# Stick-breaking attention by pairs of query blocks, and a sigmoid without GpSimd and reciprocal

## Chip, cores and metric

One core of one Trainium2 chip runs the whole program. The metric is the device time of one execution in microseconds (us); a difference is judged on the median of several runs.

## What is computed

Two layers of a streaming encoder are run on 512 prompt rows and 32 later rows ("sample") together, so 544 columns in all, with a model width of 1024. Each layer projects the residual stream into four token mixers: stick-breaking attention, retention, forgetting attention ("fox") and an indexer-selected sparse attention ("dsa"). The four results are gated, summed and projected ("merge"), then normalised, and a feed-forward network of width 2816 follows. The change touches two mixers. Cut to what matters:

```python
# stick-breaking, 4 heads of 64; 'earlier' is key position < query position
z = q @ k.T / 8
log_1mb = where(earlier, log_sigmoid(-z), 0)
after   = cumsum over keys from the end (log_1mb) - log_1mb
w       = where(earlier, exp(log_sigmoid(z) + after), 0)
y       = w @ v
# retention: the result of each head, normalised, is multiplied by a gate
y_ret = head_norm(retention(q, k, v)) * silu(ret_g)      # silu(x) = x * sigmoid(x)
```

## The kernel before

The stream is held as 128 rows by 272 columns, two halves of them, each value split into a high and a low part in a shorter float format (`split`, L694), so that a product is three matmuls of 272 columns. Most large projections use a seven-product scheme on 2 by 2 blocks (`strassen`, L784); its weight blocks are split by ScalarE (high part) and by VectorE or GpSimd (low part). A string of seven letters says which of the two makes each low part: `v` VectorE, `g` GpSimd. `SPLITS[3]` (L101) is the string for `proj2` (L919), which makes the value projection of retention, one call a layer.

**Who sets the order.** Nothing is issued in the order of the code. Every call becomes an operation with a modelled duration and a priority (its place in the code, less an offset); a list scheduler (`Plan.schedule`, L553) plays the five engines and takes on each the ready operation of highest priority. The addresses of the tiles in the on-chip memory are fitted to the lifetimes that such a play gives (`Memory.places`, L202), for several settings, of which the best by the plan is taken; an operation whose tile lies on bytes of an older one waits for the older one's readers. Where the plan sees TensorE idle, dummy matmuls of a tile called `idle` are put in (L635). So any change of an operation gives a new order of everything behind it. In the profile all operations have the line of the loop that issues them (L659, L657 for the dummies), so the rows are read by tile names.

**Banks.** The eight PSUM banks have fixed users (L107): `z`, two banks, holds the scores of all mixers; `d`, four banks, the projections; `a` the weighted sums of values; `p` transposes.

**Stick-breaking** (`stick`, L1434). The loop at L1439 takes the four query blocks of 128 in turn, and for each the two head parities `s`. The key blocks up to the query's own are taken from the last to the first, in units of up to two. A unit fills one `z` bank: a mask matmul where it holds the diagonal block, then for each key block and each of two heads two matmuls of 128 columns (L1458, high and low part of the keys). `stick_unit` (L1421) makes the log terms: Abs, Exp and Ln on ScalarE, one operation on VectorE, then the split into `hl` by ScalarE and GpSimd. Cumulative sums are matmuls into the same bank (L1467): of a block with itself by a triangle (`trin`), with every later key block by minus ones (`onen`), two parts each, 256 columns. A last Exp on ScalarE makes the weights `sw`, and after both parities the products with the values go to bank `a` (L1480), j from 0 up, for each head in turn. A unit also places two steps of the top-k selection of the dsa mixer (L1462), VectorE work on the tile `score`. After the four blocks one more unit serves the sample rows.

**Retention's gate** (`silu`, L1553). For each of two row blocks and two column halves, a projection lies in a `d` bank; ScalarE makes exp(-x) into `se`, GpSimd adds 1, VectorE takes the reciprocal, and VectorE multiplies with the bank's x into `sg`, which frees the bank.

Of the kernel before, what the change touches and what calls it, by code (L numbers as in the profile page):

```python
# [14 lines left out]
AF = mybir.ActivationFunctionType  # L15
OP = mybir.AluOpType
# [81 lines left out]
GROUPS = ((0, 6), (6, 8), (14, 8))  # L98
CORNER = ("vv",) * 12
PIECES = ([(0, 512, "v"), (512, 1024, "v")], [(0, 512, "a"), (512, 768, "a"), (768, 1024, "g")], [(0, 1024, "v")])  # L100
SPLITS = ("vvvvvvv", "vvvvvvv", "vvvvvvv", "vgvgvgv")  # L101
RESIDUAL = 2
SLACKS = (400, 100, 0)
FITS = ((10.0, 5.0), (5.0, 5.0), (10.0, 2.0), (10.0, 10.0))
# [560 lines left out]
class Build:  # L665
# [253 lines left out]
    def proj2(self, col, names):  # L919
# [3 lines left out]
        at = lambda c, h: out[:, c, h * HB:(h + 1) * HB]  # L923
        ps = self.strassen(r, 4, self.xt, None, SPLITS[3], "d", (at(0, 1), at(1, 0), at(1, 1)))[0]
        self.ev(at(0, 0), ps, eng="s")
# [508 lines left out]
    def stick(self, q, qb, k, svt):  # L1434
        nc = self.nc
        ks = self.k_parts(k, "sk")
        v, vs = svt
        y = self.fm("y_sb")
        for i in range(4):  # L1439
            blocks = list(range(i, -1, -1))  # L1440
            units = [tuple(blocks[a:a + 2]) for a in range(0, len(blocks), 2)]
            W = {}
            for s in range(2):
                r = slice(s * 64, s * 64 + 64)
                later = []
                for un in units:
                    n = 256 * len(un)
                    z = self.tps("sz")
                    first = True
                    if i in un:  # L1450
                        nc.tensor.matmul(z[:, :256], self.B["ident"],
                                         self.B["sbmask"][:, None, :].to_broadcast([128, 2, 128]), start=True,
                                         stop=False, skip_group_check=True)
                        first = False
                    for x, j in enumerate(un):
                        for p in range(2):
                            c = (2 * x + p) * 128
                            self.z(z[:, c:c + 128], q, ks, 2 * p + s, slice(i * 128, (i + 1) * 128),  # L1458
                                   slice(j * 128, (j + 1) * 128), first, True)
                            first = False  # L1460
                    hl = self.stick_unit(z, n)
                    self.select(SELECT[1])  # L1462
                    own = [(hl, 256 * x) for x in range(len(un))]
                    for x, j in enumerate(un):
                        for src, a, lhs in [(*own[x], self.trin)] + [(*b, self.onen) for b in later + own[:x]]:
                            for part in range(2):
                                nc.tensor.matmul(z[:, 256 * x:256 * x + 256], lhs, src[:, part, a:a + 256], start=False,  # L1467
                                                 stop=True, skip_group_check=True)
                    later = later + own
                    w = self.w512("sw")  # L1470
                    nc.scalar.activation(w[:, :n], z[:, :n], AF.Exp)
                    for x, j in enumerate(un):
                        W[s, j] = (w, 256 * x)
            o = self.aps("so")
            for p in range(2):
                for s in range(2):
                    h = 2 * p + s
                    for j in range(i + 1):
                        w, a = W[s, j]
                        nc.tensor.matmul(o[:, h * 128:(h + 1) * 128], v[:, j, p * 128:(p + 1) * 128],  # L1480
                                         w[:, a + p * 128:a + (p + 1) * 128], start=j == 0, stop=j == i)
            self.ev_heads(y, o, i * 128, 128)

        kc = self.cache_k("cache_sb_k", 384, NKS)
        nc.vector.tensor_copy(kc[:, :, PAST:NKS], k[:, :, T:NT])
        vc = self.cache_v("cache_sb_v", 256)
        nc.vector.tensor_copy(vc[:32, 2, :], vs)
        z = self.tps("szs")
        nc.tensor.matmul(z[:, 256:384], self.B["ident"], self.B["sbmask_s"], start=True, stop=False,
                         skip_group_check=True)  # L1490
        for j in range(3):
            for p in range(2):
                c = j * 128 + p * 64
                nc.tensor.matmul(z[:, c:c + 64], kc[:, p, j * 128:(j + 1) * 128], qb[:, p].rearrange("r s q -> r (s q)"),
                                 start=False, stop=True, skip_group_check=True)
        hl = self.stick_unit(z, 384)
        for j in range(3):
            for b in range(j, 3):
                for part in range(2):
                    nc.tensor.matmul(z[:, j * 128:(j + 1) * 128], self.trin if b == j else self.onen,  # L1500
                                     hl[:, part, b * 128:(b + 1) * 128], start=False, stop=True, skip_group_check=True)
        w = self.w512("sws")
        nc.scalar.activation(w[:, :384], z[:, :384], AF.Exp)
        self.pv_sample(w.rearrange("p (b q) -> p b q", q=128), lambda kr, j, p: vc[:kr, j, p * 128:(p + 1) * 128], y, 128)
        return y
# [35 lines left out]
    def retention(self):  # L1541
        nc, l = self.nc, self.l
        cs = self.fm("cs")
        a, b = CONST_AT["cos"][0], CONST_AT["sin"][1]
        nc.sync.dma_start(cs.rearrange("p a b -> p (a b)"), self.consts_dram[:, a:b])
        q = self.rotary(self.proj(COL["ret_q"], "rq0"), cs)
        k = self.rotary(self.proj(COL["ret_k"], "rk0", 0.125), cs)
        vf = self.proj2(COL["ret_v"], "rv")
        v, vs = self.tm(vf, "rvt", True, None)
        sg = self.fm("sg")  # L1550
        se = self.fm("se")

        def silu(c, h, ps):  # L1553
            cs = slice(h * HB, (h + 1) * HB)
            nc.scalar.activation(se[:, c, cs], ps, AF.Exp, scale=-1.0)
            nc.gpsimd.tensor_scalar(se[:, c, cs], se[:, c, cs], 1.0, None, op0=OP.add)
            nc.vector.reciprocal(se[:, c, cs], se[:, c, cs])
            nc.vector.tensor_tensor(sg[:, c, cs], se[:, c, cs], ps, op=OP.mult)

        for c in range(2):  # L1560
            a = COL["ret_g"] + c * 128
# [3 lines left out]
        y = self.fm("y_ret")  # L1565
# [39 lines left out]
        for c in range(4):  # L1605
            cc = slice(c * 128, (c + 1) * 128)
            A = self.w512("A", (128, 2, 2, 128))
            for s in range(2):
                r = slice(s * 64, s * 64 + 64)
                z = self.tps("rz")  # L1610
# [9 lines left out]
            o = self.aps("ro")  # L1620
            for p in range(2):
                if c:
                    nc.tensor.matmul(o[:, p * 128:(p + 1) * 128], qd[:, p], S[:, p], start=True, stop=False)
                for s in range(2):
                    h = 2 * p + s
                    nc.tensor.matmul(o[:, h * 64:(h + 1) * 64], A[:, s, p], v[:, c, h * 64:(h + 1) * 64],
                                     start=not c, stop=not c or s == 1)
# [10 lines left out]
        z = self.tps("rzs")  # L1638
        for p in range(2):
            nc.tensor.matmul(z[:32, p * 64:(p + 1) * 64], k[:, p, T:NT], qb[:, p].rearrange("r s q -> r (s q)"),  # L1640
                             start=True, stop=True)
# [9 lines left out]
        o = self.aps("ros")  # L1651
        for p in range(2):
            nc.tensor.matmul(o[:32, p * 128:(p + 1) * 128], qd[:, p], S[:, p], start=True, stop=False)
            for s in range(2):
                h = 2 * p + s
                nc.tensor.matmul(o[:32, h * 64:(h + 1) * 64], A[:32, p, s], vs[:, h * 64:(h + 1) * 64], start=False,
                                 stop=s == 1)
# [430 lines left out]
```

## Time and profile before

| what | us |
|---|---|
| median of 3 runs (lowest to highest) | 1942.51 (1942.05 to 1944.62) |
| the profiled execution, its own time | 1938.36 |
| span of the profiled execution, first to last instruction | 1936.6 |
| TensorE busy | 1871.6 |
| VectorE busy | 1607.1 |
| ScalarE busy | 1053.3 |
| GpSimd busy | 498.8 |

The profile comes from one execution. PE is TensorE, DVE is VectorE, ACT is ScalarE, POOL is GpSimd. Matmuls are pipelined: a matmul's record lasts longer than the time until the next one starts, so the price of one in a row of many is taken here from start to start. The dummy matmuls count as busy.

### The profile page before, as it was taken

The numbers are of one execution on the slowest core, as the hardware profiler recorded it, in microseconds if no ns is written. First come the engines' busy times: TensorE is split into PE (matmuls) and PEld (weight loads), VectorE is DVE, ScalarE is ACT, GpSimd is POOL, SyncE is SP. The second block draws the span as 40 slices with busy tenths as digits, with TensorE's granted clock in tenths as the row PEclk, the third lists the DMA queues.
The fourth block names the chain that finished last, engine by engine and source line by source line (L and its number), as shares of the span: only waits on it lengthen the run. The fifth ranks groups of instructions, "written<-read, shape, count | busy, mean of one in ns | idle before, by whom it ended". The sixth has DMA issues, their size and how long they took to land.

```text
span 1936.6 us, 39257 instructions
## 1 busy us (share of the span) xinstructions
PE 1871.6 (97%) x14658; PEld 1815.8 (94%) x14658; DVE 1607.1 (83%) x3566; ACT 1053.3 (54%) x2183; POOL 498.8 (26%) x500
## 2 busy tenths in 40 slices
PE   9999999999999999999999999999999999999997
PEld 8998898999999999999989989999999999999996
DVE  5988768887879989988789796687788799899875
ACT  4465533555637656556465563365556475565552
POOL 0343031143441111321413421312434301114101
PEclk9999999999999999999999999999999999999999
DMA  8222243667542587776413222346665237777741
GB/s 229 79 64 81 55 101 75 153 142 163 145 124 77 135 195 174 170 180 169 130 23 95 60 84 68 78 107 159 151 154 155 86 86 169 188 174 175 171 114 47
DMA packets 387423, 241.38 MB, mean 125 GB/s; under 512 B 27272, under 2 KB 363576, under 8 KB 386976
## 3 DMA queue, kind: packets, MB, share of 16 engines
q1 hardware_dynamic: 361888, 193.78, 36.2%
q0 software_dynamic: 25344, 45.10, 13.8%
q8 instruction: 115, 1.88, 0.4%
q14 instruction: 76, 0.62, 0.1%
HBM read 183.69 MB, written 7.82 MB: 99 GB/s over the span
## 4 chain that ended last, share of the span: by engine, by line
PE 71%; DVE 17%; DMA 5%; ACT 4%; issue 3%; POOL 1%; SPq 1%; POOLq 0%; ACTq 0%; DVEq 0%
PE bank L659 70%; DVE wop L659 3%; DMA ws<-wa 3%; DVE lnw L659 2%; DVE y L659 2%; DVE wsum L659 1%; DVE wlo L659 1%; DVE st L659 1%; DVE q L659 1%; DVE score L659 1%; DVE fu L659 1%; SPq L659 1%; DVE su L659 0%; DVE sv L659 0%; ACT wop L659 0%
## 5 line engine op out<-in xcount | busy, mean ns | idle before, releaser
L659 PE MATMUL bank<-T,wop 128*128 128x272 f32 x3456 | 460.6, 289 | 4.6 <-DVE su L659 3.1
L659 PEld LDWEIGHTS bank<-T,wop 128*128 128x128 f32 x3456 | 443.3, 188 | 7.1 <-DVE su L659 4.3
L659 PE MATMUL bank<-h0hi,wop 128*128 128x272 f32 x1152 | 244.9, 291 | 0.3 <-DVE acc L659 0.3
L659 PEld LDWEIGHTS bank<-h0hi,wop 128*128 128x128 f32 x1152 | 190.0, 188 | 3.6 <-DVE acc L659 0.5
L659 POOL DMA_DIRECT2D wt<-raw x88 | 76.6, 870 | 370.8 <-DVE wop L659 68.2
L659 POOL DMA_DIRECT2D ws<-wa x88 | 76.9, 874 | 352.7 <-DVE wop L659 114.8
L659 ACT ACTIVATE wop<-raw 128x512 fp32r<-128x512 f32 (+1 forms) x176 | 108.9, 620 | 107.1 <-PE bank L659 96.2
L659 PE MATMUL bank<-h0lo,wop 128*128 128x272 f32 x576 | 165.7, 288 | 0.0
L659 PE MATMUL bank<-q,wop 128*128 128x272 f32 x1176 | 153.0, 290 | 4.4 <-DVE su L659 2.6
L659 PEld LDWEIGHTS bank<-q,wop 128*128 128x128 f32 x1176 | 148.8, 189 | 7.5 <-DVE su L659 3.6
L659 DVE TENSOR_TENSOR wop<-raw,wop 128x512 fp32r<-128x512 f32 (+1 forms) x176 | 126.0, 718 | 31.1 <-ACT wop L659 30.5
L659 ACT ACTIVATE wop<-wsum 128x512 fp32r<-128x512 f32 (+1 forms) x176 | 109.1, 620 | 73.7 <-PE bank L659 46.5
L659 PE MATMUL bank<-h0hi,whi 128*128 128x272 f32 (+1 forms) x480 | 146.0, 304 | 2.3 <-ACT h0hi L659 2.3
L659 DVE TENSOR_TENSOR wlo<-raw,whi 128x1024 fp32r<-128x1024 f32 (+1 forms) x92 | 123.7, 1351 | 27.8 <-PE bank L659 12.7
L659 PE MATMUL bank<-h1hi,whi 128*128 128x272 f32 (+1 forms) x480 | 142.3, 296 | 1.1 <-DVE iq L659 1.1
L659 ACT ACTIVATE whi<-raw 128x1024 fp32r<-128x1024 f32 (+1 forms) x92 | 95.5, 1049 | 87.2 <-PE bank L659 46.6
L659 PE MATMUL bank<-h0hi,wlo 128*128 128x272 f32 (+1 forms) x480 | 139.3, 290 | 2.0 <-DVE wlo L659 2.0
L659 PE MATMUL bank<-h0lo,whi 128*128 128x272 f32 (+1 forms) x480 | 139.2, 290 | 2.0 <-DVE h0lo L659 2.0
L659 DVE TENSOR_TENSOR wop<-wsum,wop 128x512 fp32r<-128x512 f32 (+1 forms) x176 | 122.2, 694 | 22.8 <-ACT wop L659 22.0
L659 PE MATMUL bank<-h1lo,whi 128*128 128x272 f32 (+1 forms) x480 | 138.5, 289 | 0.5 <-DVE h1lo L659 0.5
L659 PE MATMUL bank<-h1hi,wlo 128*128 128x272 f32 (+1 forms) x480 | 138.6, 289 | 0.0
L659 PE MATMUL bank<-h1hi,wop 128*128 128x272 f32 x576 | 121.4, 289 | 0.0
(452 smaller groups left out, 5076.7 us busy)
## 6 DMA issues: line engine op xcount, KB each, us to landing
raw<-in_w_in_dram SPq DMA_DIRECT2D x46, 512.0 KB, 3.8
ws<-wa POOLq DMA_DIRECT2D x80, 256.0 KB, 4.4
wt<-raw POOLq DMA_DIRECT2D x80, 256.0 KB, 4.0
raw<-in_w_ffn_in_dram SPq DMA_DIRECT2D x76, 256.0 KB, 3.6
raw<-in_w_in_dram SPq DMA_DIRECT2D x68, 256.0 KB, 3.5
wa<-in_w_ffn_in_dram SPq DMA_DIRECT2D x38, 256.0 KB, 3.5
ws<-in_w_ffn_in_dram SPq DMA_DIRECT2D x38, 256.0 KB, 2.9
wt<-in_w_ffn_in_dram SPq DMA_DIRECT2D x38, 256.0 KB, 4.2
```

What stands on the lines that cost most here:

```text
L659: call(*a, **k)
```

## The change

The query blocks are taken in pairs: one unit is one key block against both blocks of the pair, 256 query columns for each of two heads; a key block that lies behind the first query block of the pair serves the second alone (`lo = 1`, 128 columns). The units are four key blocks for the second pair and two for the first, for each parity. In `silu` the add and the reciprocal become Ln(1 + e) and Exp(-...) on ScalarE, in place. `SPLITS[3]` becomes all `v`.

```diff
-SPLITS = ("vvvvvvv", "vvvvvvv", "vvvvvvv", "vgvgvgv")
+SPLITS = ("vvvvvvv", "vvvvvvv", "vvvvvvv", "vvvvvvv")
...
-        for i in range(4):
-            blocks = list(range(i, -1, -1))
-            units = [tuple(blocks[a:a + 2]) for a in range(0, len(blocks), 2)]
+        for i0 in (0, 2):
             W = {}
             for s in range(2):
                 later = []
-                for un in units:
-                    n = 256 * len(un)
+                for j in range(i0 + 1, -1, -1):
+                    lo = 1 if j > i0 else 0
+                    w = 256 - 128 * lo
+                    n = 2 * w
                     z = self.tps("sz")
+                    zv = z[:, :n].rearrange("k (p q) -> k p q", p=2)
                     first = True
-                    if i in un:
-                        nc.tensor.matmul(z[:, :256], self.B["ident"],
+                    if j >= i0:
+                        nc.tensor.matmul(zv[:, :, :128], self.B["ident"],
...
-                    for x, j in enumerate(un):
-                        for p in range(2):
-                            c = (2 * x + p) * 128
-                            self.z(z[:, c:c + 128], q, ks, 2 * p + s, slice(i * 128, (i + 1) * 128),
-                                   slice(j * 128, (j + 1) * 128), first, True)
-                            first = False
+                    for p in range(2):
+                        self.z(z[:, p * w:(p + 1) * w], q, ks, 2 * p + s, slice((i0 + lo) * 128, (i0 + 2) * 128),
+                               slice(j * 128, (j + 1) * 128), first, True)
+                        first = False
                     hl = self.stick_unit(z, n)
                     self.select(SELECT[1])
-                    own = [(hl, 256 * x) for x in range(len(un))]
-                    for x, j in enumerate(un):
-                        for src, a, lhs in [(*own[x], self.trin)] + [(*b, self.onen) for b in later + own[:x]]:
-                            for part in range(2):
-                                nc.tensor.matmul(z[:, 256 * x:256 * x + 256], lhs, src[:, part, a:a + 256], start=False,
-                                                 stop=True, skip_group_check=True)
-                    later = later + own
-                    w = self.w512("sw")
-                    nc.scalar.activation(w[:, :n], z[:, :n], AF.Exp)
+                    for src, a, lhs in [(hl, lo, self.trin)] + [(*x, self.onen) for x in later]:
+                        sw = 256 - 128 * a
+                        for part in range(2):
+                            nc.tensor.matmul(zv[:, :, w - sw:], lhs,
+                                             src[:, part, :2 * sw].rearrange("k (p q) -> k p q", p=2), start=False,
+                                             stop=True, skip_group_check=True)
+                    later.append((hl, lo))
+                    e = self.w512("sw")
+                    nc.scalar.activation(e[:, :n], z[:, :n], AF.Exp)
+                    W[s, j] = (e, w, lo)
...
+            for i in (i0, i0 + 1):
+                o = self.aps("so")
                 for p in range(2):
                     for s in range(2):
                         h = 2 * p + s
                         for j in range(i + 1):
+                            e, w, lo = W[s, j]
+                            a = p * w + (i - i0 - lo) * 128
+                            nc.tensor.matmul(o[:, h * 128:(h + 1) * 128], v[:, j, p * 128:(p + 1) * 128], e[:, a:a + 128],
+                                             start=j == 0, stop=j == i)
+                self.ev_heads(y, o, i * 128, 128)
...
             nc.scalar.activation(se[:, c, cs], ps, AF.Exp, scale=-1.0)
-            nc.gpsimd.tensor_scalar(se[:, c, cs], se[:, c, cs], 1.0, None, op0=OP.add)
-            nc.vector.reciprocal(se[:, c, cs], se[:, c, cs])
+            nc.scalar.activation(se[:, c, cs], se[:, c, cs], AF.Ln, bias=1.0)
+            nc.scalar.activation(se[:, c, cs], se[:, c, cs], AF.Exp, scale=-1.0)
             nc.vector.tensor_tensor(sg[:, c, cs], se[:, c, cs], ps, op=OP.mult)
```

## Rows read from the trace of the kernel before

**Rows 1.** The page's part 1: busy time, share, instructions.

```profile
PE 1871.6 (97%) x14658; PEld 1815.8 (94%) x14658; DVE 1607.1 (83%) x3566; ACT 1053.3 (54%) x2183; POOL 498.8 (26%) x500
```

**Rows 2.** Windows of 40 us: length, busy PE, PEld, DVE, ACT, POOL, clock, DMA.

```profile
120.00:160.00 40.00, 40.00 (x317) 36.97 (x316) 33.12 (x78) 27.31 (x50) 11.28 (x10) 1.00 0.27 81
160.00:200.00 40.00, 37.18 (x296) 34.63 (x295) 37.63 (x124) 21.08 (x57) 12.53 (x11) 1.00 0.33 88
200.00:240.00 40.00, 37.44 (x271) 33.93 (x270) 29.20 (x119) 20.30 (x62) 0.69 (x2) 0.96 0.12 30
```

**Rows 3.** Chain that ended last, 85 to 170 us: start, us, what.

```profile
98.74 56.40 PE bank L659 x444
```

**Rows 4.** Groups of instructions on PE, stick-breaking: names, shape, count, busy and mean.

```profile
L659 PE MATMUL bank<-sq,sk 128*128 128x128 f32 x80 | 19.6, 282 | 0.0
L659 PE MATMUL bank<-sq,skl 128*128 128x128 f32 x80 | 19.1, 276 | 0.0
L659 PE MATMUL bank<-hl,trin 128*128 128x256 f32 x80 | 18.3, 300 | 0.5 <-ACT hl L659 0.5
L659 PE MATMUL bank<-hl,onen 128*128 128x256 f32 x80 | 13.3, 280 | 0.0
```

**Rows 5.** Timeline of PE: thirteen matmuls of 128 columns; first, and the one behind.

```profile
133.79 0.28 PE L659 MATMUL bank<-sq,skl 128*128 128x128 f32 x1
...
135.24 0.34 PE L659 MATMUL bank<-h0hi,whi 128*128 128x272 f32 x1
```

**Rows 6.** Timeline of PE: five matmuls of 256 columns, and the one behind.

```profile
107.44 0.52 PE L659 MATMUL bank<-hl,trin 128*128 128x256 f32 x3
107.81 0.40 PE L659 MATMUL bank<-hl,onen 128*128 128x256 f32 x2
108.04 0.29 PE L659 MATMUL bank<-h1hi,whi 128*128 128x272 f32 x1
```

**Rows 7.** Timeline of PE: matmuls of 512 columns, the first and fourth of four.

```profile
50.10 0.39 PE L659 MATMUL bank<-ikh,iq 128*128 128x512 f32 x1
...
50.80 0.39 PE L659 MATMUL bank<-ikl,iq 128*128 128x512 f32 x1
```

**Rows 8.** Timeline of ACT: the first step of a pair of units, and the next pair's.

```profile
134.88 0.60 ACT L659 ACTIVATE sa<-bank 128x512 f32<-128x512 f32 x1 [0.58 <-PE bank L659]
...
144.89 0.60 ACT L659 ACTIVATE sa<-bank 128x512 f32<-128x512 f32 x1 [0.37 <-PE bank L659]
```

**Rows 9.** The tiles sw and fk: duration min/median/max, first and last start, forms.

```profile
L659 PE MATMUL bank<-sw,svt x160: 270/275/378, 96.8 to 1121.4; 128*128 128x128 f32 x160
L659 ACT ACTIVATE fk<-fk x16: 613/628/634, 152.5 to 1125.6; 64x512 fp32r<-64x512 f32 x16
```

**Rows 10.** The tile se, the same columns.

```profile
L659 ACT ACTIVATE se<-bank x8: 397/397/401, 284.3 to 1252.4; 128x272 f32<-128x272 f32 x8
L659 POOL TENSOR_SCALAR se<-se x8: 889/894/1191, 284.8 to 1252.9; 128x272 f32<-128x272 f32 x8
L659 DVE RECIPROCAL se<-se x8: 1846/1852/1855, 285.7 to 1253.8; 128x272 f32<-128x272 f32 x8
```

**Rows 11.** Chain that ended last, 234 to 300 us.

```profile
294.60 1.85 DVE se L659
...
296.89 3.14 PE bank L659 x21
```

**Rows 12.** Waits of PE: total, times, longest.

```profile
PE bank L659 <- DVE sg L659: 1.4, 2, 1.2
```

**Rows 13.** Groups of instructions on ACT, by shape.

```profile
L659 ACT ACTIVATE su<-su 128x272 f32<-128x272 f32 x70 | 30.1, 430 | 29.4 <-DVE su L659 29.2
```

**Rows 14.** Weight splits: POOL and DVE groups, and a timeline row of DVE.

```profile
L659 POOL TENSOR_TENSOR wop<-ws,wop 128x512 fp32r<-128x512 f32 x2 | 2.5, 1270 | 0.0
L659 DVE TENSOR_TENSOR wop<-ws,wop 128x512 fp32r<-128x512 f32 x78 | 54.1, 694 | 13.3 <-ACT wop L659 13.1
255.30 1.78 DVE L659 TENSOR_TENSOR wop<-wsum,wop 128x512 fp32r<-128x512 f32 x1 [0.29 <-ACT wop L659]
```

More of the change, by code (lines that the diff above doesn't have):

```diff
@@ L1438, in stick @@
         y = self.fm("y_sb")
-        for i in range(4):
-            blocks = list(range(i, -1, -1))
-            units = [tuple(blocks[a:a + 2]) for a in range(0, len(blocks), 2)]
+        for i0 in (0, 2):
             W = {}
             for s in range(2):
-                r = slice(s * 64, s * 64 + 64)
                 later = []
-                for un in units:
-                    n = 256 * len(un)
+                for j in range(i0 + 1, -1, -1):
+                    lo = 1 if j > i0 else 0
+                    w = 256 - 128 * lo
+                    n = 2 * w
                     z = self.tps("sz")
+                    zv = z[:, :n].rearrange("k (p q) -> k p q", p=2)
                     first = True
-                    if i in un:
-                        nc.tensor.matmul(z[:, :256], self.B["ident"],
+                    if j >= i0:
+                        nc.tensor.matmul(zv[:, :, :128], self.B["ident"],
                                          self.B["sbmask"][:, None, :].to_broadcast([128, 2, 128]), start=True,
@@ L1469, in stick @@
-                    later = later + own
-                    w = self.w512("sw")
-                    nc.scalar.activation(w[:, :n], z[:, :n], AF.Exp)
[L1472 to L1481, printed above, removed]
@@ L1482, in stick @@
-            self.ev_heads(y, o, i * 128, 128)
+                    for src, a, lhs in [(hl, lo, self.trin)] + [(*x, self.onen) for x in later]:
[4 more added lines that the diff above has]
+                                             stop=True, skip_group_check=True)
@@ new lines, in stick @@
+                    later.append((hl, lo))
[4 more added lines that the diff above has]
+                o = self.aps("so")
+                for p in range(2):
+                    for s in range(2):
+                        h = 2 * p + s
+                        for j in range(i + 1):
+                            e, w, lo = W[s, j]
[3 more added lines that the diff above has]
+                self.ev_heads(y, o, i * 128, 128)
```

## The prediction

> **What bounds the kernel now.** I read the page's busy times first. TensorE is busy 1871.6 of 1936.6 us; VectorE has 17% free, ScalarE 46%, GpSimd 74% [rows 1]. So work taken off TensorE counts most, and work moved between the other engines counts where TensorE waits for it. TensorE's 65 us of idle time are also the measure of what a new order of the same work can win or lose.
>
> Then the windows around the first layer's attention. From 120 to 160 us, where stick-breaking runs, TensorE is busy all 40.00 us: dense projections fill what stick-breaking leaves. From 160 to 240, where the fox and dsa mixers follow, it is busy 37.18 and 37.44, and VectorE is at 37.63 in the first of the two [rows 2]: there the mixers' own chains set part of the pace. The chain that ended last agrees: one piece of 56.40 us and 444 matmuls on TensorE without a wait goes through stick-breaking [rows 3]. A matmul saved there should bring fox forward by its price.
>
> Last, retention's gate. Its reciprocal stands on the chain, and TensorE resumes only after it, at 296.89 [rows 11].
>
> **The change part by part.** All counts are for both layers.
>
> *Scores.* Before there are 80 + 80 matmuls of 128 columns [rows 4]; by the loops, 10 pairs of query and key block times 2 parities, 2 heads, 2 parts and 2 layers, which is the same 160. After, each parity has six units: two with 128 columns a head (the last key block of each pair) and four with 256. That is 2 x 2 x 2 x 2 x 2 = 32 matmuls of 128 columns and 64 of 256. Price: thirteen of 128 columns take 133.79 to 135.24, 0.1115 us each [rows 5]; five of 256 take 107.44 to 108.04, 0.120 each [rows 6]. So 160 x 0.1115 = 17.8 us become 32 x 0.1115 + 64 x 0.120 = 11.3: **-6.6 us**. The width is almost free up to 256 columns; it is the number that costs.
>
> By the Trainium skill ("TensorE: Matmul & The Clock Gate", Back-to-back issue gap) the isolated gap grows with the columns, 56 ns at 128 and 109 at 256, so half as many matmuls of double width would cost the same and the term would be near 0. The rows disagree: 111 ns against 120. The same section's 81 ns for a sustained stream at 128, of loads and matmuls, is nearer to them.
>
> *Cumulative sums.* 80 + 80 matmuls of 256 columns [rows 4] become, per parity and layer, 12 of 256 and 14 of 512 (first pair: 1 triangle of 256, 1 of 512, 1 row of ones of 256; second: 1 triangle of 256 and 3 of 512, ones 3 of 256 and 3 of 512; times two parts), so 48 and 56. At 512 columns three steps take 0.70 us, 0.233 each [rows 7]. 19.2 us become 5.8 + 13.0 = 18.8: **-0.4 us**. The output of the narrower sums lies in two runs of 128; no row has that form in fp32, and I bound it by the two widths it lies between, 0.1115 and 0.120.
>
> *What stays.* Mask matmuls (8 a layer), units (12 a layer, four of 256 and eight of 512 columns), their ScalarE, VectorE and GpSimd steps, the calls of the selection (24 steps) and the 160 value matmuls [rows 9] are the same in number and size. Nothing is moved past a DMA queue; no DMA is added.
>
> *What moves.* Both blocks of a pair now end together. Behind the last weights there were 12 products of two value matmuls each (three heads of four key blocks; the heads go in order, and the second waits for the last unit). There will be 9 for the pair's first block and, in the same single `a` bank, 16 for its second: 26 matmuls more. At 0.112 each, as for the scores of the same width [rows 5], 2.9 us come later in each layer. I cost it at nothing: the product of stick-breaking is read only in the merge, and dense projections fill TensorE meanwhile [rows 2]. If that cover is gone it is +2.9 a layer.
>
> *How much of the 7.0 arrives.* Upper end: all, since TensorE is full in that stretch. Lower end: 0, if the fox stage is held by VectorE. Between them lies the stick-breaking chain itself: two units share the two `z` banks, and a pair takes 134.88 to 144.89, 10.0 us [rows 8]; its 16 score matmuls are 1.8 of them, and 8 wide ones would be 1.0. If only the unit that waits for the other gains, half arrives, 3.5. I take all, because the chain that ended last runs on TensorE there and a pair's two score bursts follow each other on it.
>
> *The gate.* Exp 0.397, add 0.894, reciprocal 1.852 in a row [rows 10] become Exp 0.397, Ln 0.43, Exp 0.43 (the row of a 272-column ScalarE pass in place [rows 13]): 1.9 us less between projection and product, eight times. VectorE loses 8 x 1.85 = 14.8 us of work, GpSimd 7.2, ScalarE gets 16 x 0.43 = 6.9. TensorE waited 1.4 us in all for this product [rows 12]; it cannot win more from this edge: **-1.4 us**, at least 0. Behind the two new passes on ScalarE's queue stand weight splits; with 46% free [rows 1] I cost that at nothing, and at one pass, +0.43 a layer, if a split is late.
>
> *Retention's value weights.* Six low parts leave GpSimd (1.27 each) for VectorE (0.69) [rows 14]: 4.2 us more for VectorE, in total still 10.6 less. One split beside such a GpSimd pass took 1.78 instead of 0.69 [rows 14], so a block may even be ready 1.1 sooner. Blocks are prepared ahead of their product: 0, between -1.1 and +0.7 a layer.
>
> **Sum.** -6.6 - 0.4 - 1.4 = -8.4 us. Against the profiled execution's own time, 1938.36, that is 1930.0. That execution lies 4.15 under the median of the runs, 1942.51; carried over, **1934.1**.
>
> **Rivals.** A measurement of this kernel tells 0.2% from no change, 3.9 us: faster is under 1938.6, slower over 1946.4.
>
> *A, half arrives* (chain of the two banks): -3.5 - 1.4, 1937.6. For it: the 10.0 us a pair. Against: TensorE without idle time in that window.
>
> *B, fox doesn't start or run sooner* because VectorE, 37.63 of 40 [rows 2], is the bound from 160 us on: only the gate's 1.4 stays, 1941.1. Against: the next window has VectorE at 29.20, so a lead is kept once its backlog ends.
>
> *Columns set the price*, as the skill's page has it: also 1941.1, from the rows hardly likely.
>
> *C, the other side: the tiles of a pair live longer and fox's key tiles wait for them.* Four `hl` of 4 KB a partition and eight `sw` of 2 KB must live together, 32 KB where one block needed about 16 (two `hl` and four `sw`). If the fitted addresses put fox's key copies on them, these can't start at 152.5 [rows 9] but only when the last pair has ended, up to a pair's 10.0 us later [rows 8]. That is 20 in all; with the 8.4 won, 1942.5 + 20 - 8.4 = 1954.1. It decides from 4.2 us a layer on, and turns slower from 6.2. For it: memory is fitted afresh. Against: fits that come late lose by the plan, and dense work covers some of it.
>
> That the change doesn't do what it says I count as nothing: the numbers of matmuls follow from the loops.
>
> **How the numbers follow.** Forecast 0.53, A 0.17, B 0.12, columns 0.03, C 0.15. The likeliest gives 1934.1. Faster: the forecast and most of A, 0.53 + 0.13 = 0.66. Same: the rest of A, B, columns and a small C, 0.04 + 0.12 + 0.03 + 0.03 = 0.22. Slower: 0.12. The range: a new order may win a tenth of TensorE's 65 us of idle time, down to 1927; up, it takes in A, B and a C of some 6 us a layer, to 1945. The full C and luck below stay out.
>
> **What would show it.** Right: the group of sq and sk has 16 matmuls a tile at 128 columns and 32 at 256, their stretch stays without idle time, and fk's first score matmuls come 3.5 us earlier in each layer; no wait for sg on PE; se without POOL and DVE; `wop` without POOL. A: pairs take 9.5 us or more and PE shows idle time or dummies between 90 and 160. B: fox starts earlier and its end doesn't. C: ACT fk starts later than 152.5 against the end of its projection, and waits for PE. The forecast is wrong if merge and feed-forward, which the change does not touch, differ in length by more than the attention stages do: then the new order, not the parts costed here, made the time.

## The result, and the profile after

| | before | after |
|---|---|---|
| median of 3 runs (lowest to highest), us | 1942.51 (1942.05 to 1944.62) | 1956.41 (1954.33 to 1956.76) |
| span of the profiled execution, us | 1936.6 | 1954.9 |

The ratio is 1.0066 [1.0043, 1.0089]: the kernel became 13.9 us slower, where 8.4 us less were forecast, and outside the forecast's range. (A ratio is formed from runs made beside each other on one chip; it can differ by 0.1% from that of two medians.)

The page of after, part 1, answers to [rows 1]; the two windows to the second and third of [rows 2], with the same columns:

```profile
PE 1881.3 (96%) x14467; PEld 1816.9 (93%) x14467; DVE 1591.2 (81%) x3564; ACT 1059.5 (54%) x2197; POOL 490.4 (25%) x486
```

```profile
160.00:200.00 40.00, 36.86 (x274) 33.33 (x274) 36.74 (x121) 23.16 (x59) 7.67 (x7) 0.96 0.35 103
200.00:240.00 40.00, 38.15 (x268) 34.05 (x268) 32.53 (x130) 19.43 (x59) 0.62 (x3) 0.96 0.11 30
```

TensorE has 191 instructions fewer (120 matmuls of scores and sums, 71 dummies) and is busy 9.7 us longer. So the work that was taken off is not what made the time.

**The parts costed did come off.** Groups on PE, after, the counterparts of [rows 4]:

```profile
L659 PE MATMUL bank<-sq,sk 128*128 128x256 f32 x32 | 9.2, 310 | 0.3 <-ACT sw L659 0.3
L659 PE MATMUL bank<-sq,sk 128*128 128x128 f32 x16 | 4.3, 290 | 0.0
L659 PE MATMUL bank<-hl,trin 128*128 128x512 f32 x32 | 13.5, 422 | 0.8 <-POOL hl L659 0.8
L659 PE MATMUL bank<-hl,onen 128*128 128x512 f32 x24 | 6.9, 394 | 0.0
L659 PE MATMUL bank<-hl,onen 128*128 128x256 f32 x32 | 6.3, 280 | 0.0
```

The counts are those of the prediction. The price of one wide score matmul is seen from start to start in the timeline of PE, after (start, us, what):

```profile
100.29 0.37 PE L659 MATMUL bank<-sq,sk 128*128 128x256 f32 x1
100.50 0.28 PE L659 MATMUL bank<-sq,skl 128*128 128x256 f32 x1
100.62 0.28 PE L659 MATMUL bank<-sq,sk 128*128 128x256 f32 x1
100.74 0.28 PE L659 MATMUL bank<-sq,skl 128*128 128x256 f32 x1
100.85 0.38 PE L659 MATMUL bank<-sw,svt 128*128 128x128 f32 x2
```

The first of a burst takes 0.21 us, the others 0.12. Added up from start to start over all of them, scores fell from 18.7 to 13.1 us and sums from 20.8 to 20.2: 6.2 us less, of the 7.0 expected. Most of the 0.8 that is lacking is one wait: the step that starts at 1078.70 takes 0.90 us, of which TensorE stands idle for 0.62 behind that score matmul. Without it the scores fell by 6.4. The Trainium skill ("TensorE: Matmul & The Clock Gate", Back-to-back issue gap) gives an isolated gap that doubles from 128 to 256 columns; the trace has medians of 111 to 113 ns and of 117 to 120, so that rival of the prediction falls.

**Where the time is.** I price each matmul by its width, as from start to start in a row without a wait (0.112 us up to 128 columns, 0.127 at 272, 0.227 at 512, where [rows 7] have 0.233; in between in proportion), and split the time from TensorE's first matmul to its last:

| us of the profiled execution | before | after | difference |
|---|---|---|---|
| all matmuls at those prices | 1816.6 | 1809.2 | -7.4 |
| dummies | 24.2 | 16.3 | -7.9 |
| the rest, at 2.4 GHz (waits, first matmuls of a burst) | 77.0 | 92.7 | +15.7 |
| the rest, in stretches at 1.2 GHz | 4.7 | 22.7 | +18.0 |

So TensorE's own work did fall by 7.4 us, and waits grew by twice that; the 7.9 us fewer of dummies were not forecast. Outside the last 15 us of the program it ran at 1.2 GHz for 51.2 us, against 10.2 before. A window of 40 us around the end of the first layer, the first row of before, the second of after (columns as in [rows 2]):

```profile
960.00:1000.00 40.00, 35.84 (x287) 33.66 (x286) 34.09 (x86) 24.63 (x57) 6.26 (x8) 1.00 0.18 51
```

```profile
960.00:1000.00 40.00, 32.92 (x244) 30.68 (x245) 28.09 (x71) 20.09 (x44) 11.44 (x6) 0.91 0.15 41
```

TensorE was idle for 7.1 of these 40 us, not 4.2, and the clock granted fell to 0.91. The last line of the table is in part a draw. The mean granted clock is on record for nearly every execution: the profiled one of before, 1938.36 us, had 0.995, which only 3 of the 95 executions of before timed in this study reach (0.988 to 0.995, on the mean 0.9915; 1937.5 to 1951.4 us); the three of after had 0.985, 0.987 and 0.985. As a mean of the two levels, 0.9915 is 33 us at 1.2 GHz, and after's 0.9857 is 56. Between typical executions the difference is thus some 23 us, not the 41 of these two.

The waits of PE, after (total, times, longest):

```profile
PE bank L659 <- DVE pT L659: 9.7, 7, 3.5
PE bank L659 <- DVE su L659: 7.2, 11, 1.5
PE bank L659 <- POOL lnw L659: 5.5, 4, 3.2
PE bank L659 <- ACT lnw L659: 4.7, 2, 3.2
PE bank L659 <- DVE lnw L659: 2.5, 1, 2.5
```

Before they were 4.8 and 5.7 for the first two and 3.7 for `lnw` together. `pT` are the transposed weights of fox and dsa; `lnw` belongs to the normalisations, which the change does not touch. The wait for `sg` [rows 12] is gone.

**Stick-breaking became shorter, what follows it longer by more.** I take stick-breaking from the first matmul of sq and sk to the end of the last of sws (its sample unit), and the mixers from there to the end of the last product pT,vv of dsa. The two stages of the first layer as windows (columns as in [rows 2]), before:

```profile
89.80:169.60 79.80, 79.37 (x641) 75.51 (x638) 65.49 (x146) 54.08 (x106) 38.15 (x25) 1.00 0.29 84
169.60:260.70 91.10, 84.27 (x641) 77.83 (x639) 70.86 (x247) 43.04 (x120) 15.03 (x16) 0.98 0.25 63
```

After:

```profile
90.60:164.40 73.80, 73.37 (x562) 68.52 (x560) 60.32 (x133) 54.60 (x105) 40.02 (x27) 1.00 0.23 66
164.40:264.60 100.20, 93.07 (x679) 85.58 (x678) 78.76 (x261) 44.17 (x123) 10.39 (x14) 0.95 0.28 76
```

The same windows for the selection's tile `score` alone (length, busy VectorE, then as before), before and after:

```profile
89.80:169.60 79.80, 32.02 (x81) 1.00 0.29 84
169.60:260.70 91.10, 9.20 (x18) 0.98 0.25 63
```

```profile
90.60:164.40 73.80, 29.80 (x73) 1.00 0.23 66
164.40:264.60 100.20, 13.12 (x26) 0.95 0.28 76
```

The stage is 6.0 us shorter. It holds 79 matmuls fewer, of which the pairs account for 60 (32 scores and 28 sums); the others, and selection steps, now run among fox and dsa: 38 matmuls more there, 3.9 us more of selection, and 9.1 us more of time. Together +3.1. In the second layer -9.1 and +13.4, together +4.3. Over half of what the mixers grew by is work of TensorE that changed its place, projections and ten transposes of fox's keys a layer: at the prices above they hold 4.9 us more of matmuls in the first layer and 9.9 in the second. So the length of one stage alone is neither loss nor gain. In the sum over both layers, +7.4, TensorE's work is -3.1, the rest at 2.4 GHz +7.7 and at 1.2 GHz +2.8. The lead is gone inside fox, as first and last starts in the first layer show, before and after:

```profile
L659 PE MATMUL bank<-fk,fq x16: 305/366/505, 163.8 to 198.2; 128*128 128x128 f32 x4, 128*128 128x256 f32 x4, 128*128 128x384 f32 x4, 128*128 128x512 f32 x4
L659 PE MATMUL bank<-pT,fvt x80: 270/275/377, 177.7 to 211.9; 128*128 128x128 f32 x80
L659 PE MATMUL bank<-pT,vv x80: 270/275/421, 225.9 to 260.4; 128*128 128x128 f32 x80
```

```profile
L659 PE MATMUL bank<-fk,fq x16: 278/366/482, 161.0 to 197.9; 128*128 128x128 f32 x4, 128*128 128x256 f32 x4, 128*128 128x384 f32 x4, 128*128 128x512 f32 x4
L659 PE MATMUL bank<-pT,fvt x80: 270/275/377, 179.6 to 212.6; 128*128 128x128 f32 x80
L659 PE MATMUL bank<-pT,vv x80: 270/275/422, 227.8 to 264.3; 128*128 128x128 f32 x80
```

Fox's scores begin at 161.0 instead of 163.8, its first products already 1.9 us late, and dsa ends 3.9 us late. The two attention stages account for 7.4 of the 18.3 us between the spans. In the other 10.9 us TensorE's work is 4.6 and the dummies are 8.0 us less; the rest at 2.4 GHz is 8.2 us more, and the rest at 1.2 GHz 15.2. Outside these stages after ran at 1.2 GHz for 34.2 us, the profiled execution of before not at all. The waits for `lnw` grew by 9.0: they lie in the normalisations before the feed-forward (3.2 at once in the first layer, 2.5 in the second) and at the end of the first layer, inside the window of 40 us shown above (3.2 and 1.6).

### The profile page after: what moved, and what is told of

Same layout as the page of the kernel before. It is cut to its first block, busy times and chain, and to the rows that moved or that the text cites. A ratio compares the mean times of both kernels' runs of the same rounds, so it can differ in the third digit from the quotient of the medians.

```text
span 1954.9 us, 38923 instructions
## 1 busy us (share of the span) xinstructions
PE 1881.3 (96%) x14467; PEld 1816.9 (93%) x14467; DVE 1591.2 (81%) x3564; ACT 1059.5 (54%) x2197; POOL 490.4 (25%) x486
## 4 chain that ended last, share of the span: by engine, by line
PE 31%; DVE 11%; DMA 3%; ACT 3%; issue 2%; POOL 0%; SPq 0%; POOLq 0%; ACTq 0%; DVEq 0%
PE bank L659 30%; DVE wop L659 2%; DMA ws<-wa 1%; DVE lnw L659 1%; DVE wlo L659 1%; DVE y L659 1%; DVE wsum L659 1%; DVE st L659 0%; DVE q L659 0%; DMA raw<-in_w_ffn_in_dram 0%; DMA raw<-in_w_ffn_out_dram 0%; DVE fu L659 0%; ACT whi L659 0%; DVE T L659 0%; DMA cs<-in_consts_dram 0%
## 5 line engine op out<-in xcount | busy, mean ns | idle before, releaser
L659 ACT ACTIVATE wop<-wsum 128x512 fp32r<-128x512 f32 (+1 forms) x176 | 109.1, 620 | 80.7 <-PE bank L659 53.5
L659 DVE TENSOR_TENSOR wlo<-raw,whi 128x1024 fp32r<-128x1024 f32 (+1 forms) x92 | 119.3, 1301 | 33.5 <-PE bank L659 15.3
```

Source lines behind the costliest of these rows:

```text
L659: call(*a, **k)
```

## Experiments

Each ratio is against runs of before on the same chip at the same time.

### Each part alone, planned anew

Of the diff, e1 has the hunk of `stick` alone, e2 that of `silu`, e3 the line of `SPLITS`.

> Stick-breaking by pairs alone, gate and value weights as before. Theory O (the new order and the newly fitted addresses that it brings cost more than the saved matmuls; the order with pairs meets waits that the plan doesn't have, and the granted clock falls to 1.2 GHz behind them): at least +6 us on the kernel before, with over 30 us of the span at 1.2 GHz, as the changed kernel has 51. Theory S (stick-breaking itself is slower, through its tail or its longer-lived tiles): its last score matmul and the start of fox come later than before against the start of stick-breaking. Theory P (each part pays as costed): -7 us.

> The gate by Exp, Ln and Exp alone. Theory O: a size that does not follow from the part, anywhere from -6 to +8 us, since the order is planned anew. Theory P: -1.4 us, and no wait of TensorE for sg left. If the gate is what costs in the changed kernel: +10 us or more.

> The six low parts of retention's value weights on VectorE alone. Theory P: 0, between -2 and +1.4 us. Theory O: again a size that the part cannot give, between -6 and +8 us.

Measured: e1 1965.08 us, 1.0109 [1.0090, 1.0129]; e2 1936.12, 0.9962 [0.9940, 0.9984]; e3 1950.71, 1.0044 [1.0028, 1.0060]. The pairs alone lose 21 us; the gate gains 7 where 1.4 were possible; six small subtractions moved from one engine to another cost 7. No operation costed above has these sizes. Each edit gave a new order, so order and operations had to be parted.

### The scores' saving in the order of before, and other plans

e5 plans the kernel before and then does not issue 64 of the 160 score matmuls; e6 and e7 force one setting of the address fit on before and after, e4 and e8 others on after:

```diff
-            for call, a, k in self.ops[i].calls:
+            for call, a, k in () if i in self.skip else self.ops[i].calls:
...
-FITS = ((10.0, 5.0), (5.0, 5.0), (10.0, 2.0), (10.0, 10.0))
+FITS = ((10.0, 5.0),)
```

> The kernel before with its plan, order and addresses untouched, but 64 of the 160 score matmuls of stick-breaking (the low part of the keys, in all pairs of blocks but two) are planned and then not issued. So it leaves out a correction of the scores, and has as many matmuls fewer as the change. If the saving is real and only the new order loses it (theory O): -7 us, between -4 and -9, at the price of the rows, 64 x 0.112. If the saving itself is hidden, because the chains of the mixers or VectorE set the pace (rival B): 0, within 2 us.

> The kernel before, with no operation changed, planned with the setting (10, 5), whose planned end is 1.3 us behind that of the chosen (10, 2). Theory O (any new order and placing costs or gives several us that no operation accounts for): a time that differs from the kernel before by over 4 us, either way. If order and addresses don't matter beyond the plan's own measure: +1.3 us, within 2.

> The changed kernel planned with (10, 5); its planned end is 2.5 us behind that of the chosen (5, 5). Theory O: by over 3 us another time than the changed kernel's 1956, either way; the idle time of TensorE at the layer norms (three waits of 2.5 to 3.2 us in the changed kernel) is not there or of another size. If stick-breaking itself is slower (S): 1956 to 1959, and the loss stands in the attention stages.

> The changed kernel, but with the addresses fitted by the setting that the plan chose for the kernel before (spare 10, margin 2) and not by (5, 5), which it chose for the changed kernel. Operations are the same; order and addresses differ. Theory O: another time, by over 3 us, most likely less than the changed kernel's; 1942 or below if the setting is the whole cause. Theories S and P: the same time as the changed kernel, within 3 us, since the parts are the same.

> The changed kernel planned with (10, 10); its planned end is 4.3 us behind that of the chosen (5, 5). Theory O: by over 3 us another time than 1956, either way. Theory S: 1956 to 1961.

Measured: e5 1947.50, 1.0016 [0.9997, 1.0035]; e6 1950.26, 1.0030 [1.0015, 1.0046]; e7 1959.05, 1.0065 [1.0042, 1.0088]; e4 1958.52, 1.0070 [1.0045, 1.0096]; e8 1950.63, 1.0041 [1.0023, 1.0059].

e5 is the forecast's first term without a new order, and the kernel's time shows nothing of it. TensorE's work fell by 7.2 us, but stick-breaking became only 1.6 and 1.3 us shorter in the two layers: beside its matmuls 2.0 and 2.3 us more went by. In the first layer dsa ended where it had, its mixers at 1.2 GHz for 6.8 us instead of 3.4; in the second, with 3.4 instead of 6.8, the stretch from the first score to the end of dsa became 3.2 us shorter. So some 3 of the 7 us came through the attention in this execution, and were lost behind it: the stages outside are 11.6 us longer, 7.8 of them the rest at 1.2 GHz, which before's profiled execution does not have there. The mean clock of e5's ten executions is 0.9897, that of before beside them 0.9914. First layer of e5, against fk 163.8 and vv 260.4 before:

```profile
L660 PE MATMUL bank<-fk,fq x16: 305/365/505, 162.3 to 196.6; 128*128 128x128 f32 x4, 128*128 128x256 f32 x4, 128*128 128x384 f32 x4, 128*128 128x512 f32 x4
L660 PE MATMUL bank<-pT,vv x80: 270/275/547, 224.5 to 260.3; 128*128 128x128 f32 x80
```

e6 has the very operations of before in another order and loses 0.3%, at a mean clock of 0.992, no lower than before's. After loses with all four settings.

### Does the clock make the loss?

e9 puts 812 more dummies into after, at the 58 longest waits of its trace; e10 599 at 48 waits of before, e11 531 at 43 waits of e2:

```diff
-            for j in range(count.get(i, 0)):
+            for j in range(count.get(i, 0) + EXTRA.get(i, 0)):
```

> The changed kernel with its order and addresses untouched; 812 dummy matmuls of 56 ns are put in at the 58 places where its profiled execution shows TensorE late by over 0.4 us, each place filled up to 0.2 us short of the wait. Theory C (the waits that the plan doesn't know let the granted clock fall to 1.2 GHz, 51 us of the span, and what is lost there is over half of the difference to the kernel before): less than 25 us of the span at 1.2 GHz, and 8 to 18 us less time than the changed kernel's 1956. Theory W (the waits themselves are the loss, the clock only marks them): the same time within 3 us, whatever the clock does, or longer by the dummies.

> The kernel before, treated in the same way: 599 dummies at 48 places of its own profiled execution. It had 10 us of the span at 1.2 GHz in that execution, and the spread of its runs (1938 to 1950) suggests more in others. Theory C: 2 to 6 us less, and a narrower spread. Theory W: the same within 2 us.

> The gate by Exp, Ln and Exp alone (1936.1), with 531 dummies at 43 places of its profiled execution, which had 41 us of the span at 1.2 GHz. Theory C: 6 to 15 us less, and so the fastest kernel here, at 1922 to 1930. Theory W: 1936 within 3 us.

Measured: e9 1960.58, 1.0086 [1.0069, 1.0103]; e10 1955.69, 1.0072 [1.0048, 1.0096]; e11 1947.62, 1.0019 [1.0004, 1.0034]. e10 and e11 became slower than the kernels that they fill (before, and e2 at 0.9962); e9 is not told from after (1.0066), since their intervals overlap. In e9 the time at 1.2 GHz fell from 51.2 to 30.7 us and the loss there from 22.7 to 10.3, the waits at 2.4 GHz from 92.7 to 53.6; but dummies took 57.1 us more, so the sum rose by 5.6. Dummies are no remedy. How much of the 13.9 us the clock would give back if it stayed up for free, these runs do not tell. The executions of before give an estimate: over the 95 of them, 0.001 less of the mean clock goes with 1.3 us more of time, so that the 0.0058 between before and after would go with some 8 us. It says nothing on which of the two brings the other. And the clock is not all: e3 and e6 had 0.9914 and 0.9920, as before had, and are slower by 0.44% and 0.30%.

### What holds the mixers, and is the loss the pairs' own?

e12 plans the kernel before and does not issue the top-k steps; e13 leaves the 64 matmuls of e5 out as well. e14 and e15 change the offset of one priority, in before and in e1:

```diff
+            nc.skip.update((len(nc.ops) - 2, len(nc.ops) - 1))
...
-HIPRI = 220
+HIPRI = 230
```

> The kernel before with its plan untouched; the top-k steps on VectorE (MAX8 and MATCH_REPLACE on the tile score) are planned but not issued, so the dsa mixer attends without its selection. It takes some 40 us or more a layer of VectorE's work out of stick-breaking, fox and dsa. If VectorE holds fox and dsa (rival B): fox+dsa shorter by 5 us or more in each layer (91.1 and 86.3 before), the kernel faster by 10 us or more. If the mixers' own chains hold them: fox+dsa within 3 us of before.

> As e12, and the 64 score matmuls of e5 not issued either (the low part of the keys left out for all but the first key block); the plan is still that of before. If VectorE's backlog held back what e5 saved: now the saving arrives, 5 to 7 us less than e12. If the mixers' chains or the order hold it: within 2.5 us of e12, as e5 stood to before.

> The kernel before with the priority offset HIPRI 230 for 220: the same operations in a new order. If the time is a draw of the order: anywhere from -8 to +8 us of before, the attention stages included. If the order before is a special one: +3 to +8, as e3 and e6.

> Stick-breaking by pairs alone (e1) with HIPRI 230: the same operations as e1 in a new order. If the loss belongs to the pairs (selection and dense work pushed into fox and dsa): fox+dsa again 96 us or more in each layer, stick-breaking 72 to 78, the kernel 5 us or more over e14. If e1's +21 was one unlucky order: within 3 us of e14 or under it.

Measured: e12 1941.56, 0.9980 [0.9965, 0.9995]; e13 1937.24, 0.9963 [0.9949, 0.9977]; e14 1959.76, 1.0071 [1.0048, 1.0094]; e15 1970.46, 1.0132 [1.0116, 1.0147].

First the window from 85 to 265 us, before and e12 (columns as in [rows 2]):

```profile
85.00:265.00 180.00, 172.44 (x1345) 161.47 (x1345) 143.12 (x416) 99.41 (x232) 53.49 (x42) 0.99 0.27 72
```

```profile
85.00:265.00 180.00, 172.46 (x1336) 161.65 (x1335) 100.77 (x287) 99.23 (x232) 52.58 (x42) 0.98 0.27 72
```

VectorE lost 42 us of work in this window and TensorE does the same in it. Fox and dsa took 92.8 and 84.0 us (before 91.1 and 86.3), at 1.2 GHz for 6.8 and 3.4 us of it (before 3.4 and 6.8). So at the order of before the selection's load on VectorE does not set their pace. The kernel as a whole gained 0.2%, clear of the noise; the trace, of the slowest of its ten executions, does not show where. With VectorE freed, the 64 matmuls bring 4.3 us between the medians (0.17% between the ratios, whose intervals overlap): less than the 5 to 7 expected if VectorE held them back, more than the 2.5 if not. In the traces the attention of both layers is 6.5 us shorter in e13 than in e12, 3.0 of it the rest at 1.2 GHz; the 3.5 left are near the 3.2 that came through in e5. That speaks against VectorE's backlog, on one execution each.

e14 has the operations of before and is 0.7% slower. The kernel before is thus a good one among the orders run here. And e15 stands 0.6% over e14: with this setting, too, the pairs lose.

### The gate and the value weights in the order of before

e16 plans as before; when the operations are issued, Ln and Exp on ScalarE stand at the places of the add and the reciprocal. In e17 the six low parts of retention's value weights are issued to VectorE as well. e18 is e2 with the other priority offset.

```diff
-            nc.gpsimd.tensor_scalar(se[:, c, cs], se[:, c, cs], 1.0, None, op0=OP.add)
-            nc.vector.reciprocal(se[:, c, cs], se[:, c, cs])
+            e, act = se[:, c, cs], nc.real.scalar.activation
+            nc.gpsimd.tensor_scalar(e, e, 1.0, None, op0=OP.add)
+            nc.swap[len(nc.ops) - 1] = [(act, (e, e, AF.Ln), dict(bias=1.0))]
+            nc.vector.reciprocal(e, e)
+            nc.swap[len(nc.ops) - 1] = [(act, (e, e, AF.Exp), dict(scale=-1.0))]
```

> The kernel before, planned as before; only when the operations are issued, the gate's add on GpSimd and reciprocal on VectorE are replaced, at their places, by Ln and Exp on ScalarE. By the prediction's term: 0 to 2 us faster than before, the wait of TensorE for sg (1.4) gone. If the gate itself is worth what e2 showed: 5 us or more faster.

> As e16, and the six low parts of retention's value weights go from GpSimd to VectorE at their places, too. By the prediction's term (0, between -2.2 and +1.4 in both layers): within 2 us of e16. If e3's +7 was the splits themselves: 4 us or more over e16.

> The gate alone (e2) with HIPRI 230: a new order of the same operations. If e2's gain belongs to the gate: 4 us or more under e14 (1959.8). If it was the order: anywhere within 10 us of e14, on either side.

Measured: e16 1943.01, 1.0011 [0.9996, 1.0026]; e17 1946.80, 1.0021 [1.0006, 1.0036]; e18 1955.73, 1.0071 [1.0055, 1.0088]. The tile se in e16 (duration min/median/max, first and last start):

```profile
L661 ACT ACTIVATE se<-se x16: 413/422/434, 287.1 to 1258.0; 128x272 f32<-128x272 f32 x16
L661 DVE TENSOR_TENSOR sg<-se,bank x8: 427/431/439, 289.2 to 1258.6; 128x272 f32<-128x272 f32 x8
```

The steps are as short as costed (0.42 each, 0.43 taken) and the wait for `sg` is gone, but no time is: e16 is within its uncertainty of before, and at the other priority offset the gate (e18) stands where e14 stood without it. So the 7 us of e2 came with its order. It is still the fastest full version run here, faster than both kernels: before with the new gate and nothing else.

### All orders together

Lengths in us of stick-breaking and of fox with dsa, first and second layer, from the profiled executions. These are single draws: that of before is among its fastest, that of e8 its fastest, those of e2, e4, e7, e14, e15 and after are their slowest.

| kernel | ratio | stick 1 | mixers 1 | stick 2 | mixers 2 | sum |
|---|---|---|---|---|---|---|
| before | 1 | 79.8 | 91.1 | 81.7 | 86.3 | 338.9 |
| e2 (gate) | 0.9962 | 79.8 | 92.2 | 81.7 | 86.4 | 340.1 |
| e3 (value weights) | 1.0044 | 79.7 | 91.3 | 85.3 | 87.8 | 344.1 |
| e6 (fit) | 1.0030 | 79.8 | 91.8 | 85.3 | 88.2 | 345.1 |
| e14 (priority) | 1.0071 | 81.2 | 91.5 | 80.7 | 93.5 | 346.9 |
| e18 (gate, priority) | 1.0071 | 79.8 | 93.1 | 80.7 | 94.1 | 347.7 |
| after | 1.0066 | 73.8 | 100.2 | 72.6 | 99.7 | 346.3 |
| e1 (pairs) | 1.0109 | 73.8 | 98.6 | 72.6 | 98.7 | 343.7 |
| e4 (after, fit) | 1.0070 | 72.9 | 105.0 | 72.7 | 101.6 | 352.2 |
| e7 (after, fit of e6) | 1.0065 | 72.3 | 101.2 | 76.2 | 101.3 | 351.0 |
| e8 (after, fit) | 1.0041 | 77.2 | 95.9 | 73.9 | 96.3 | 343.3 |
| e15 (pairs, priority of e14) | 1.0132 | 73.9 | 100.1 | 72.0 | 100.9 | 346.9 |

Two things are seen. Without the pairs, five new orders of nearly the same work lie between 0.38% under and 0.71% over before. With the pairs, stick-breaking is shorter in each of six orders than in any without, and fox with dsa longer: the mean sum is 347.2 us (343.3 to 352.2) against 343.8 (338.9 to 347.7) without pairs, ranges that overlap, though TensorE has 7 us less to do. And wherever the same setting was run with and without the pairs, with them was slower: 1.09% (e1 against before, each as the plan chose), 0.61% (e15, e14), and with the gate and the value weights, too, 0.70% (e4 against before, whose setting it has) and 0.35% (e7, e6; their intervals overlap). But most of that loss lies outside fox and dsa. Between the profiled executions, the attention stages account for 4.8 of the 25.4 us from before to e1, for none of the 10.2 from e14 to e15, and for 5.9 of the 10.7 from e6 to e7.

## Why the prediction was wrong

**What held.** The counts of matmuls; the terms of the scores and the sums (-6.6 and -0.4 forecast, -5.6 and -0.6 measured, the first -6.4 without its one wait; the prediction's 11.3 should read 11.2); the step times of the gate, the wait for `sg` gone. The value weights cost little at the order of before: e17 over e16 is 0.1% of the ratio, 2 us, and 3.8 us between the medians, with intervals that overlap; the bounds were -2.2 and +1.4.

**The step that failed** is "How much of the 7.0 arrives": "I take all, because the chain that ended last runs on TensorE there". In the order of before nothing of it is seen in the kernel's time (e5, 1.0016 [0.9997, 1.0035]). Even in the stretch without idle time only 1.6 and 1.3 us of 3.6 a layer came out at the end of stick-breaking, not far from the half that rival A gave for its two banks; the others came back as time beside the matmuls. A row of TensorE without a wait says that TensorE is full, not that what is taken off it comes out at the end of the stage. And the 3 us that did come out do not show in the whole; how far the lower clock of e5 hides them is open. The same goes for the gate's -1.4: the wait that was seen disappeared and the time did not (e16).

The Trainium skill ("Perfetto Trace Analysis", Identifying the Most-Contended Engine) says to optimise the most contended engine first, and to judge TensorE by the operations that it does against its peak and by the share of its weight loads, 94% here [rows 1]. The prediction took TensorE for that engine. e5 shows 7.2 us less on it and a time that is not shorter; e12 shows 42 us less on the second busiest engine in the first layer's attention, TensorE busy there as before, and 0.2% of the time.

**The term that was missing** is the new order. The prediction gave it a tenth of TensorE's 65 us of idle time, as a gain. Measured on orders whose operations hardly differ, it goes from -7 us to +14, and four of five are losses. That is more than everything I had costed, and the forecast had only one arm of it. Its last sentence named the sign by which this would show: the stages outside the attention, +10.9 us, differ by more than the attention stages, +7.4. The sign is there, but between these two executions it is above all the clock's: of what grew outside, 15.2 us are the rest at 1.2 GHz.

**What the pairs add** beyond the draw: a loss in four of four comparisons, one of them within the noise. Shown is that in every order with pairs the shorter stick-breaking stage passes matmuls and selection steps on to fox and dsa, which grow by more than it shrinks against before, and by as much where e15 is set against e14. That the passing on is the cause of the loss is not shown: work that changes its place is no loss by itself, e12 says that the selection alone does not set the mixers' pace, and from e14 to e15 the whole loss lies outside these stages. I had costed "What moves" at nothing with the dense projections as cover; that cover itself was what moved.

**The rivals.** A is nearest in the share that came out of stick-breaking in e5. B's sign is there in the first layer: fox starts 2.8 us sooner and dsa ends 3.9 later. In the second layer fox starts 76.1 us after the first score instead of 73.9. B's reason, VectorE as the bound, is not borne out by e12, and its time, 1941.1, is 15 us short. C gave 1954.1, near to the result, and its sign is there in the first layer of after, too:

```profile
157.62 1.94 ACT L659 ACTIVATE fk<-fk 64x512 fp32r<-64x512 f32 x3 [2.81 <-PE bank L659]
```

Fox's key copies start at 157.6 for 152.5, after ScalarE stood idle for 2.81 us until TensorE, then in the value products of the last pair, released it. Yet fox's scores begin sooner than before, so the price of up to 20 us that C needs for its time is not seen. What part of the loss this wait has was not tested.

**Open:** where outside the attention the pairs lose, and by what; what each mixer waits for when neither TensorE's work nor the selection sets its length; and how much of the loss is the time at 1.2 GHz, some 23 us more in typical executions, which comes with more waits and could not be taken away without cost.

## To carry to other kernels

Where a scheduler re-plans everything after each edit, first measure what a new order alone does, by two or three neutral settings, and make that spread the width of the forecast. Then test an edit in the old order, by planning with the old operations and issuing the new ones or leaving the saved ones out: if it is worth nothing there, what its result after planning shows is the new order. Time saved on a full engine need not arrive: see in the old order how much sooner the stage and the one behind it end before taking it as a gain. And before two traces are compared, look at the granted clock of many executions of each kernel: a trace is one draw.

## What the runs showed of the hardware that was not expected

A score matmul of 256 columns costs some 6 ns more than one of 128 (medians 117 to 120 ns against 111 to 113), but at the head of a burst 0.20 us against 0.14. Time at 1.2 GHz, outside the last 15 us, varied between the profiled executions from 10 to 55 us. It varies within one kernel as well: the mean granted clock of the executions of before goes from 0.988 to 0.995, and their times spread over 14 us (1937.5 to 1951.4), more than most edits here were worth.
